# Joined later differences, a joined sixth product, sooner rows, high parts ahead of low parts, and a fourth row squared on two engines, in a hybrid decoder layer

## The chip, the core and the metric

The kernel runs on one core of one Trainium2 chip. The metric is device time in microseconds (us) of one execution; three timed runs of the kernel before gave 1316.51, 1317.4 and 1314.1 us, median 1316.51.

A core has five engines that run side by side, each through its own queue in order. PE (TensorE) multiplies and writes to PSUM banks; DVE (VectorE), ACT (ScalarE) and POOL (GpSimd) work on elements; SP (SyncE) issues most DMAs here. An instruction waits on semaphores for what it needs, and everything behind it on its engine waits with it. So the order in which the program gives instructions to each engine is part of the design.

## The reference

One decoder layer over 2048 positions of width 1024, in float32:

```python
xn = rms_norm(h, ln_g)
proj = jnp.einsum('bsd,de->bse', xn, w_in)            # 1024 -> 6 x 1024
b_gate, c_gate, x_conv, g_conv, x_lru, g_lru = jnp.split(proj, splits, axis=-1)
y_conv = short_conv_mixer(b_gate, c_gate, x_conv, conv_w)
y_conv = headwise_rms_norm(y_conv, N_CONV_HEADS, conv_out_g) * jax.nn.silu(g_conv)
y_lru = rg_lru_mixer(x_lru, lru_conv_w, lru_conv_b, w_a, b_a, w_i, b_i, lam)
y_lru = headwise_rms_norm(y_lru, N_LRU_HEADS, lru_out_g) * jax.nn.silu(g_lru)
y = jnp.concatenate([y_conv, y_lru], axis=-1)
h = h + jnp.einsum('bse,ed->bsd', y, w_out)           # 2048 -> 1024
return rms_norm(h, final_g)
```

`rg_lru_mixer` holds a width-4 convolution, two block-diagonal maps with sigmoids (the "gates") and a linear recurrence over the positions. Nearly all of the arithmetic is in the two projections.

## The kernel before

**Products.** Every float32 operand is split into a high part (a cast to fp32r, on ACT) and a low part (value minus high part, on DVE or POOL). A product of two 128x128-blocked operands is then three matmuls: high x high, high x low, low x high (`mm`, L1009). Each matmul has a 128x128 stationary piece S and a 128x512 moving piece T. Four such (index `j`, over 128 rows each) make one product of 12 matmuls.

**Steps.** `steps` (L268 to L272) lists 64 units of work, n = 0 to 63: for the first half of the positions (h = 0) 24 steps, kinds "l" (inputs of the recurrence), "a" and "b" (the convolution's), then 24 for the second half (h = 1), then 16 of kind "o" for the output projection. A step makes a 2x2 block of results by seven products in place of eight, with sums and differences of the blocks (indices 0 to 6). The S side of a step is prepared during the step before it by the eight small functions of `s_plan` (L192), called as `prep(n + 1, s - 1)`: index 6 of the list is `hi(5)`, the high part of product 5, which is called at the start of step n itself. Later halves load S again from DRAM by `s_loads`. The T side (differences of the x blocks, or of w_out's) lasts for a whole set of steps; sets open at n = 24, 48 and 56. The class `Change` (L435) builds the next set while the last steps of the old one run: `of_x` for n = 24, `of_w` for 48 and 56, one call per slot with a counter `q`. `sixth` (L473) makes the T operand of product 6 out of two earlier differences: DVE subtracts, `cut` casts on ACT and subtracts on DVE.

**Slots.** The loop at L1231 runs a step in seven slots of one product each, in the order 0, 6, 1, 3, 2, 4, 5, where the 6 is the sixth product of the step before (`pend`, L1296), added to a bank of that step. Products 0, 1, 2 and 5 add to one bank "A"; after products 0, 1 and 2 ACT copies the running sum out (L1315 `q1`, L1318 `u2`, L1321 `rr`), and the next product on "A" must wait for the copy. `put(which, bank, other)` consumes a finished block. The step that opens a set (n = 24, 48, 56) has eight plain products; the one after it (25, 49, 57, called `late`) has the order 0, 4, 5, 1, 3, 2 (`AFTER`). There are two ways to postpone: `at(k, f)` runs f at the k-th following `tick()`, that is at a slot's start, and `defer(f)` runs f at once unless `held[0]` is a list, in which case `release()` runs it (L175 to L184).

**The first three steps** have no seven products. Steps 0 to 2 use eight products each. Step 0 is written out by hand (L1101 to L1143): four rounds `j` for banks c11 and c21, then four for c12 and c22, while x is normalised (`norm_rows`, L528), turned by PE (`turn`, L550) and split. The first four rows of 128 positions are normalised before anything else, one after the other. Steps 1 and 2 are `plain(1, ...)` and `plain(2, ...)` (L1181), 8 slots each of 12 matmuls. `bits` (L1152) is a list of 16 small functions, four for each j: the first set's differences on DVE with casts on ACT. `after1` runs two of them in each slot of plain(1), all 16. `after2` in plain(2) would run those left over; it also prepares step 3 and, from slot 4 on, T operands 3 and 6.

**Around it.** Step 0's recurrence work is on timers that run through plain(1) and plain(2): `gates(0)` and then `sigs(0)` at the first slot of plain(2), `gates(1)` and `sigs(1)` at its third. A gate is two PSUM tiles of a pool with two buffers (`pss`), which ACT reads by four sigmoids (L758), so `gates(1)` must wait for `sigs(0)`. In "o" steps of the second kind (ph = 1) partial rows lie in DRAM (`od`) and are loaded (`load`, L891) by SP as `xr`, added on DVE (L942), squared on ACT (L931). `m1` (L830) is the first tap of the short convolution, on ACT.

Of the kernel before, what the change touches and what calls it, by code (L numbers as in the profile page):

```python
# [12 lines left out]
F32 = mybir.dt.float32  # L13
# [25 lines left out]
def hymba_kernel(ctx: ExitStack, tc: tile.TileContext, x, xt, w_in, par, lamc, w_gate, w_out, final_g, out):  # L39
# [152 lines left out]
    def s_plan(n, r, dst):  # L192
# [22 lines left out]
        def lo(i, eng=None):  # L215
            low(val(i), dst[i], eng)
            if PLAIN <= n < 3 * KT:
# [8 lines left out]
                lambda: (hi(4), lo(4, g), lo(2)),  # L226
                lambda: hi(5),
                lambda: (hi(6), lo(6, g), lo(5))]
# [206 lines left out]
    class Change:  # L435
# [36 lines left out]

        def sixth(self, *js):  # L473
            for j in js:
                tt(self.r[6, j], self.r[6, j], self.r[1, j], ALU.subtract)
            self.cut([(6, j) for j in js])

        def of_x(self, q):
# [13 lines left out]
            if q == 21:  # L492
                self.sixth(0, 1)
                at(1, lambda: self.sixth(2, 3))
            self.cut({1: ((5, 0), (5, 1)), 2: ((5, 2), (5, 3)), 4: ((0, 0), (0, 1)), 5: ((4, 0), (4, 1)),
# [31 lines left out]

    def norm_rows(b):  # L528
        junk = sp.tile([P, D], F32, tag="s", name="junk")
        ss = small.tile([P, 1], F32, tag="ss", bufs=4, name="ss")  # L530
        rs = small.tile([P, 1], F32, tag="rs", bufs=4, name="rs")
        nc.scalar.activation(out=junk, in_=x0[b], func=AF.Square, accum_out=ss)
        nc.scalar.activation(out=rs, in_=ss, func=AF.Sqrt, scale=1.0 / D, bias=eps)

        def scale():
            nc.vector.reciprocal(out=rs, in_=rs)
            nc.vector.tensor_scalar(out=x0[b], in0=x0[b], scalar1=rs, scalar2=0.0,
                                    op0=ALU.mult, op1=ALU.add)

        return scale  # L540
# [280 lines left out]
    def conv_a(h, k):  # L821
# [20 lines left out]
        def put(which, bank, other):  # L842
            if which in (11, 12):
                combine(p[:, 4:4 + C] if which == 11 else p[:, 4 + C:4 + N2], bank, other)
            else:
                xx[which] = aux("xx")
                combine(xx[which], bank, other)
            if which == 12:
                at(1, lambda: tt(p[:, 4 + C:4 + N2], p[:, 4 + C:4 + N2], xx[22], ALU.mult))
            if which == 21:  # L850
                tt(p[:, 4:4 + C], p[:, 4:4 + C], xx[21], ALU.mult)
                at(1, m1)
                at(2, lambda: mj(1), lambda: mj(2), keep)
# [30 lines left out]
    def outp(ph, m):  # L884
# [29 lines left out]
        elif ph == 1 or m not in X_LATE:  # L914
            at(5, lambda: load(0))
            at(6, lambda: load(1))

# [135 lines left out]
    with tc.manual_schedule(engines={ENG.PE, ENG.Activation, ENG.DVE, ENG.Pool, ENG.SP}):  # L1053
# [7 lines left out]
        Wr.append(load_s(1))  # L1061
        for b in range(NB):
            norm_rows(b)()
        Sp = [{} for _ in range(PLAIN)]

# [34 lines left out]
        Tp[0].lo(4)  # L1100
        c11, c21 = bank(), bank()  # L1101
        scale = lambda: None
        for j in range(NB):
            if j + 1 < NB:
                first(j + 1)
                for i in (0, 4):
                    Tp[j + 1].hi(i)
                Tp[j + 1].lo(0)
                Tp[j + 1].lo(4, g)
            scale()  # L1110
            scale = norm_rows(NB + j)
            for cc, aa in ((c11, 0), (c21, 2)):
                mm(cc, Sp[0], T, aa, j, j == 0, False, k=0)
# [18 lines left out]
        for j in range(NB):  # L1132
# [4 lines left out]
            if j == 2:  # L1137
                put = lru(0, 0, 1, 1)
                put(11, c11, None)
                put(21, c21, None)  # L1140
            for cc, aa in ((c12, 0), (c22, 2)):
                mm(cc, Sp[0], T, aa, j, j == 0, False, k=3)
# [51 lines left out]
        def after1(s):  # L1194
            i = {2: 2, 3: 3, 5: 0, 7: 1}.get(s)
            if i is not None:
                s_hi(2, i)
            do_bits(2)
            if i is not None:
# [13 lines left out]
        def after2(s):  # L1213
            do_bits(2)
            if s in (1, 2, 3, 4, 6, 7):
# [15 lines left out]
        for n in range(PLAIN, N):  # L1231
# [27 lines left out]
            bk = {}  # L1259
            slots = (0, 6) + ORDER[1:] if not late else AFTER  # L1260
            for s in range(6 if late else 8 if new or last else 7):
                i = slots[s]
                place[0] = {"l": 0, "a": 7, "b": 14}.get(kind, 0) + s
                tick()
                if soon and s == 3:
# [6 lines left out]
                if late:  # L1272
                    change.slot(16 + s)
                    if s == 0:
                        prep(n, 7)
                elif n > 0 and opens(n - 2):
# [3 lines left out]
                    elif s == 2:  # L1280
                        prep(n, 7)
                elif s == 0:
                    prep(n, 6)
                elif s == 2:
                    prep(n, 7)
# [5 lines left out]
                elif s > 0:  # L1291
                    held[0] = [] if i == 2 else None
                    prep(n + 1, s - 1)
                if s == 3:
                    load_next(n + 2, 3 if late else 4)
                if s == 1 and not late:  # L1296
                    if pend is not None:
# [15 lines left out]
                if i == 0:  # L1313
                    q1 = sm_q1[0] = sm("q1")
                    nc.scalar.copy(q1, bk["A"])  # L1315
                elif i == 1:
                    u2 = sm_u2[0] = sm(("u2", "rr")[n % 2])
                    nc.scalar.copy(u2, bk["A"])  # L1318
                elif i == 2:
                    rr = sm(("rr", "u2")[n % 2])  # L1320
# [3 lines left out]
                    if late:  # L1324
                        put(12, bk["D"], rr)
                elif i == 4:
                    put(11, bk["C"], q1)
# [54 lines left out]
```

## Time and profile before

| | us |
|---|---|
| median of three runs (range) | 1316.51 (1314.1 to 1317.4) |
| the profiled execution's own time | 1314.92 |
| its span on the core | 1313.1 |
| PE busy in the span | 1289.5 |
| DVE busy | 1046.0 |
| ACT busy | 748.7 |
| POOL busy | 250.0 |

The span is cut into stages by the steps: step 0 from about 14 to 45 us, plain(1) to 67 us, plain(2) to 98 us, then steps of about 20 us each; the sets open at about 513, 991 and 1148 us. In rows of the time view the columns are start, duration, engine, line, operation, tiles written<-read, shapes, count, and in brackets the idle time of the engine before the row with what ended it. In the view of waits the columns are the waiting engine, line and what it waited for, then total us, number of times and the longest. In the view of windows each stretch has, after its length, the busy us and count for PE, weight loads, DVE, ACT and POOL, then the granted clock, the DMA share and GB/s.

### The profile page before, as it was taken

To read this page: it belongs to the slowest core of one execution; us is meant where nothing else is said; L and a number is where in the kernel's file an instruction comes from. 1 tells how busy PE (TensorE), PEld (TensorE's weight loads), DVE (VectorE), ACT (ScalarE), POOL (GpSimd) and SP (SyncE) were. 2 spreads that over 40 slices of the span, in tenths; PEclk is the share of its full clock that TensorE was granted. 3 is DMA by queue.
4 is the path that set the end of the run, shared out by engine and by line. 5 is a ranking of instruction groups with operands and counts; after the bars stand their busy time and mean duration, and the time that the engine had idled before them with its cause. 6 is when DMAs were issued, how large, how long until landed. Compare 5 with 4: busy or idle time off the path is not lost.

```text
span 1313.1 us, 16711 instructions
## 1 busy us (share of the span) xinstructions
PE 1289.5 (98%) x5688; PEld 1061.0 (81%) x5688; DVE 1046.0 (80%) x1284; ACT 748.7 (57%) x1141; POOL 250.0 (19%) x189
## 2 busy tenths in 40 slices
PE   7989999999999999999999999999999999999997
PEld 6867888888888888778888888888888888887886
DVE  6789898999999998967666666667559767649886
ACT  7576767576675667566454645454466433445443
POOL 3204243344435441001010110101011000000000
PEclk9989999999999999999999999999999999999999
DMA  7128887898989887651899999999789986697654
GB/s 294 32 90 290 290 286 264 302 350 283 345 302 329 295 301 280 207 199 33 277 318 296 340 352 333 324 355 362 236 271 339 260 261 229 249 402 273 235 179 160
DMA packets 157958, 355.29 MB, mean 271 GB/s; under 512 B 16944, under 2 KB 51760, under 8 KB 157872
## 3 DMA queue, kind: packets, MB, share of 16 engines
q1 hardware_dynamic: 153264, 338.17, 74.4%
q0 software_dynamic: 4320, 15.73, 3.1%
q8 instruction: 45, 0.74, 0.2%
q14 instruction: 41, 0.34, 0.1%
q10 hardware_dynamic: 288, 0.32, 0.1%
HBM read 217.11 MB, written 137.04 MB: 270 GB/s over the span
## 4 chain that ended last, share of the span: by engine, by line
PE 82%; DVE 8%; DMA 5%; ACT 3%; issue 2%; SPq 0%; POOL 0%; ACTq 0%; DVEq 0%
PE bank L1014 79%; DMA s<-so 2%; DVE tl L163 2%; PE gate L751 2%; DVE traw L163 1%; DMA tl<-td 1%; DMA zr<-rsd 1%; DMA xr<-od 1%; DMA fg<-in_final_g_dram 1%; DVE u L723 1%; ACT i L758 0%; DVE s L163 0%; ACT r L758 0%; ACT th L451 0%; PE tp L554 0%
## 5 line engine op out<-in xcount | busy, mean ns | idle before, releaser
L1014 PE MATMUL bank<-th,s 128*128 128x512 f32 x3632 | 1129.6, 390 | 5.7 <-ACT rr L1318 1.6
L1014 PEld LDWEIGHTS bank<-th,s 128*128 128x128 f32 x3632 | 682.7, 188 | 151.7 <-ACT rr L1318 2.5
L1014 PE MATMUL bank<-tl,s 128*128 128x512 f32 x1816 | 708.2, 390 | 1.8 <-DVE tl L163 1.6
L1014 PEld LDWEIGHTS bank<-tl,s 128*128 128x128 f32 x1816 | 341.4, 188 | 74.5 <-DVE tl L163 3.0
L163 POOL TENSOR_TENSOR s<-raw,s 128x512 fp32r<-128x512 f32 x62 | 115.1, 1870 | 231.1 <-ACT s L213 176.0
L213 ACT CAST s<-raw 128x512 fp32r<-128x512 f32 x140 | 85.4, 618 | 48.4 <-PE bank L1014 32.8
L163 POOL TENSOR_TENSOR gb<-gb,sg 128x1024 f32<-128x1024 f32 x16 | 43.4, 2712 | 335.5 <-ACT sg L682 335.5
L163 DVE TENSOR_TENSOR s<-raw,s 128x512 fp32r<-128x512 f32 (+1 forms) x125 | 91.6, 755 | 10.6 <-ACT s L1073 6.7
L163 DVE TENSOR_TENSOR s<-s,s 128x512 fp32r<-128x512 f32 x105 | 86.6, 824 | 2.1 <-ACT s L213 1.5
L163 DVE TENSOR_TENSOR tl<-traw,th 128x512 fp32r<-128x512 f32 x85 | 60.8, 748 | 19.4 <-ACT th L451 13.4
L213 ACT CAST s<-s 128x512 fp32r<-128x512 f32 x105 | 64.7, 616 | 4.3 <-DVE s L163 4.0
L723 DVE SCALAR_TENSOR_TENSOR u<-xl,pt,u 128x1024 f32<-128x1024 f32 x48 | 61.3, 1278 | 6.1 <-ACT u L719 5.5
L835 DVE SCALAR_TENSOR_TENSOR t<-p,pt,t 128x1024 f32<-128x1024 f32 x32 | 46.5, 1454 | 16.6 <-ACT t L832 15.8
L1315 ACT COPY q<-bank 128x512 f32<-128x512 f32 x58 | 33.9, 584 | 40.9 <-PE bank L1014 31.5
L163 DVE TENSOR_TENSOR st<-u,st 64x512 fp32r<-64x512 f32 x64 | 53.8, 841 | 2.0
L758 ACT ACTIVATE r<-gate,pt 64x512 f32<-64x512 f32 x64 | 43.7, 683 | 17.3 <-PE gate L751 16.5
L1318 ACT COPY rr<-bank 128x512 f32<-128x512 f32 x31 | 18.1, 584 | 53.6 <-PE bank L1014 53.3
L1318 ACT COPY u<-bank 128x512 f32<-128x512 f32 x27 | 15.8, 585 | 52.4 <-PE bank L1014 52.4
L163 DVE TENSOR_TENSOR traw<-traw 128x512 f32<-128x512 f32 x60 | 41.8, 701 | 4.7 <-DMA traw<-in_w_out_dram 3.6
L451 ACT CAST th<-traw 128x512 fp32r<-128x512 f32 x64 | 36.1, 618 | 16.1 <-DVE traw L163 14.2
L758 ACT ACTIVATE i<-gate,pt 64x512 f32<-64x512 f32 x64 | 43.8, 684 | 1.1
L1321 ACT COPY u<-bank 128x512 f32<-128x512 f32 x31 | 18.1, 585 | 43.6 <-PE bank L1014 43.5
(169 smaller groups left out, 1294.1 us busy)
## 6 DMA issues: line engine op xcount, KB each, us to landing
sd<-s SPq DMA_DIRECT2D x151, 512.0 KB
s<-sd SPq DMA_DIRECT2D x151, 512.0 KB
raw<-in_w_in_dram SPq DMA_DIRECT2D x104, 256.0 KB
raw<-yd SPq DMA_DIRECT2D x64, 256.0 KB
traw<-in_w_out_dram SPq DMA_DIRECT2D x64, 256.0 KB
so<-so SPq DMA_DIRECT2D x22, 512.0 KB
s<-so SPq DMA_DIRECT2D x22, 512.0 KB
yd<-gl SPq DMA_DIRECT2D x32, 256.0 KB
```

Source lines behind the costliest of these rows:

```text
L163: (eng or nc.vector).tensor_tensor(out=out, in0=a, in1=b, op=op)
L213: nc.scalar.copy(dst[i][0], val(i))
L451: nc.scalar.copy(self.dst[i, j][0], self.r[i, j])
L723: nc.vector.scalar_tensor_tensor(out=v["u"], in0=o1[:, 1 + j:1 + j + N2], scalar=lw[j], in1=v["u"], op0=ALU.mult, op1=ALU.add)
L751: nc.tensor.matmul(ps[j], v["gw"][n][:, j, :], v["st"][j][:, sl], start=(n == 0), stop=(n == 1))
L758: nc.scalar.activation(out=g_[hi, sl], in_=v["ps"][j][src], func=AF.Sigmoid, bias=pt[src, bias + k:bias + k + 1])
L835: nc.vector.scalar_tensor_tensor(out=tcur["t"], in0=p[:, 2 + j:2 + j + N2], scalar=cw[j], in1=tcur["t"], op0=ALU.mult, op1=ALU.add)
L1014: nc.tensor.matmul(bank, a[:, js], b, start=start and n == 0, stop=stop and n == 2, skip_group_check=more)
L1315: nc.scalar.copy(q1, bk["A"])
L1318: nc.scalar.copy(u2, bk["A"])
L1321: nc.scalar.copy(rr, bk["A"])
```

## The change

- **Later differences.** `after1` runs `bits` only in its first six slots (12 of 16), and `after2` runs one in each slot, so the four of j = 3 run in the first four slots of plain(2).
- **Sixth product.** `sixth` does all four subtractions in one call at `q == 21`, and its cut one tick later. In step 26 the order of slots is 0, 3, 6, 1, 2, 4, 5. In "o" steps after an opening one, the slot's `Change` call moves behind the copy u2 where i = 1, and the preparation of the next step behind `put` where i = 2.
- **Deferred casts.** `hi(5)` and `m1` go through `defer`; a list is now open from the start of a step's first slot, and `release()` also follows the copies q1 and u2.
- **Sooner rows.** The two `xr` loads of step 56 (ph 1, m 2) are issued three ticks earlier.
- **High parts first.** In the first of the four rounds of each half of step 0, the 12 matmuls run in an order in which those that need only T's high parts come first (`spread`).
- **Fourth row.** Of the fourth row, DVE squares one half and ACT the other; the third and fourth rows are scaled in two parts, by column blocks, and the last part of the fourth on ACT, later.

```diff
-                lambda: hi(5),
+                lambda: defer(lambda: hi(5)),
...
-        def sixth(self, *js):
-            for j in js:
+        def sixth(self):
+            for j in range(NB):
                 tt(self.r[6, j], self.r[6, j], self.r[1, j], ALU.subtract)
-            self.cut([(6, j) for j in js])
+            at(1, lambda: self.cut([(6, j) for j in range(NB)]))
...
-                self.sixth(0, 1)
-                at(1, lambda: self.sixth(2, 3))
+                self.sixth()
...
+        if halves:
+            s2 = small.tile([P, 1], F32, tag="ss", bufs=4, name="s2")
+            nc.vector.scalar_tensor_tensor(out=junk[:, C:], in0=x0[b][:, C:], scalar=1.0, in1=x0[b][:, C:],
+                                           op0=ALU.mult, op1=ALU.mult, accum_out=s2)
+            nc.vector.tensor_scalar(out=s2, in0=s2, scalar1=1.0 / D, scalar2=EPS, op0=ALU.mult, op1=ALU.add)
+            nc.scalar.activation(out=junk[:, 0:C], in_=x0[b][:, 0:C], func=AF.Square, accum_out=ss)
+            nc.scalar.activation(out=rs, in_=ss, func=AF.Sqrt, scale=1.0 / D, bias=s2)
...
-                at(1, m1)
+                at(1, lambda: defer(m1))
...
-            at(5, lambda: load(0))
-            at(6, lambda: load(1))
+            sooner = 3 if ph == 1 and m == 2 else 0
+            at(5 - sooner, lambda: load(0))
+            at(6 - sooner, lambda: load(1))
...
-        for b in range(NB):
+        for b in range(NB - 2):
             norm_rows(b)()
+        third = norm_rows(NB - 2)
+        fourth = norm_rows(NB - 1, True)
+        third(0)
+        fourth(0)
+        third(1)
...
+        def spread(order):
+            seen = []
+            for cc, i, w, t, v in order:
+                nc.tensor.matmul(cc, Sp[0][i][w][:, 0:P], T[t, 0][v], start=not any(b is cc for b in seen),
+                                 stop=False)
+                seen.append(cc)
...
+                if j == 0:
+                    fourth(1)
...
+                spread(((c11, 0, 0, 0, 0), (c11, 0, 1, 0, 0), (c21, 2, 0, 0, 0),
+                        (c11, 1, 0, 4, 0), (c11, 1, 1, 4, 0), (c21, 3, 0, 4, 0), (c21, 2, 1, 0, 0),
+                        (c11, 0, 0, 0, 1), (c21, 2, 0, 0, 1), (c11, 1, 0, 4, 1), (c21, 3, 0, 4, 1),
+                        (c21, 3, 1, 4, 0)))
...
-            do_bits(2)
+            if s < 6:
+                do_bits(2)
...
-            do_bits(2)
+            do_bits(1)
...
+            if kind != "o" and n > 1 and opens(n - 2):
+                slots = (0, 3, 6, 1, 2, 4, 5)
...
+                if i == 1 and slots[2] == 6:
+                    held[0] = []
                 tick()
...
                 if late:
-                    change.slot(16 + s)
+                    if i != 1 or kind != "o":
+                        change.slot(16 + s)
...
                 elif s == 0:
+                    held[0] = []
                     prep(n, 6)
...
-                    held[0] = [] if i == 2 else None
-                    prep(n + 1, s - 1)
+                    if i == 2 and not late:
+                        held[0] = []
+                    if i != 2 or kind != "o" or not late:
+                        prep(n + 1, s - 1)
...
                     nc.scalar.copy(q1, bk["A"])
+                    release()
                 elif i == 1:
                     u2 = sm_u2[0] = sm(("u2", "rr")[n % 2])
                     nc.scalar.copy(u2, bk["A"])
+                    release()
+                    if late and kind == "o":
+                        change.slot(16 + s)
...
+                        if kind == "o":
+                            prep(n + 1, s - 1)
```

In the diff `fourth(1)` is the part of the scale that ACT runs (`activation` with Copy and the row's factor); `scale(part)` picks half of the column blocks.

More of the change, by code (lines that the diff above doesn't have):

```diff
@@ L525, in load, with norm_rows @@
             self.loaded = max(n, self.loaded)
-    def norm_rows(b):
+    def norm_rows(b, halves=False):
         junk = sp.tile([P, D], F32, tag="s", name="junk")
@@ L531, in norm_rows, with scale @@
         rs = small.tile([P, 1], F32, tag="rs", bufs=4, name="rs")
[L532 to L538, printed above, removed]
+        if halves:
[5 more added lines that the diff above has]
+            nc.scalar.activation(out=rs, in_=ss, func=AF.Sqrt, scale=1.0 / D, bias=s2)
+        else:
+            nc.scalar.activation(out=junk, in_=x0[b], func=AF.Square, accum_out=ss)
+            nc.scalar.activation(out=rs, in_=ss, func=AF.Sqrt, scale=1.0 / D, bias=eps)
+        def scale(part=None):
+            v = x0[b]
+            if part is not None:
+                v = v.rearrange("p (i k c) -> p i k c", i=2, c=P)[:, :, 2 * part:2 * part + 2, :]
+            if part != 1:
+                nc.vector.reciprocal(out=rs, in_=rs)
+            if part == 1 and halves:
+                nc.scalar.activation(out=v, in_=v, func=AF.Copy, scale=rs)
+            else:
+                nc.vector.tensor_scalar(out=v, in0=v, scalar1=rs, scalar2=0.0, op0=ALU.mult, op1=ALU.add)
         return scale
@@ L1111, in hymba_kernel @@
             scale = norm_rows(NB + j)
+            if j == 0:
+                spread(((c11, 0, 0, 0, 0), (c11, 0, 1, 0, 0), (c21, 2, 0, 0, 0),
+                        (c11, 1, 0, 4, 0), (c11, 1, 1, 4, 0), (c21, 3, 0, 4, 0), (c21, 2, 1, 0, 0),
+                        (c11, 0, 0, 0, 1), (c21, 2, 0, 0, 1), (c11, 1, 0, 4, 1), (c21, 3, 0, 4, 1),
+                        (c21, 3, 1, 4, 0)))
+                continue
             for cc, aa in ((c11, 0), (c21, 2)):
@@ L1140, in hymba_kernel @@
                 put(21, c21, None)
+            if j == 0:
+                spread([(cc, i, w, t, 0) for t, d in ((3, 0), (5, 1)) for cc, i in ((c12, d), (c22, 2 + d))
+                        for w in range(2)] +
+                       [(cc, i, 0, t, 1) for t, d in ((3, 0), (5, 1)) for cc, i in ((c12, d), (c22, 2 + d))])
+                continue
             for cc, aa in ((c12, 0), (c22, 2)):
@@ L1291, in hymba_kernel @@
                 elif s > 0:
-                    held[0] = [] if i == 2 else None
-                    prep(n + 1, s - 1)
+                    if i == 2 and not late:
+                        held[0] = []
+                    if i != 2 or kind != "o" or not late:
+                        prep(n + 1, s - 1)
                 if s == 3:
                     load_next(n + 2, 3 if late else 4)
-                if s == 1 and not late:
+                if i == 6 and not late and s < 3:
                     if pend is not None:
```

## The prediction

> **What bounds the kernel now.** I read the page first: busy shares, then the chain.
>
> ```profile
> PE 1289.5 (98%) x5688; PEld 1061.0 (81%) x5688; DVE 1046.0 (80%) x1284; ACT 748.7 (57%) x1141; POOL 250.0 (19%) x189
> ```
>
> PE works almost throughout, and the change leaves the number of matmuls as it is. So the only time to win is PE's idle time. The chain in order of time gives the undisturbed pace, and two windows give a slow stretch and a stretch full of transfers:
>
> ```profile
> 141.75 51.71 PE bank L1014 x228
> ```
>
> ```profile
> 73.42:83.99 10.57, 6.97 (x16) 4.84 (x16) 8.46 (x12) 10.00 (x17) 0.10 (x1) 0.68 0.01 2
> ...
> 1150.00:1170.00 20.00, 20.00 (x90) 16.57 (x89) 6.49 (x10) 7.55 (x15) 0.53 (x1) 1.00 1.04 405
> ```
>
> A 128x512 matmul costs 51.71 / 228 = 0.227 us. The first window holds 16 matmuls, worth 16 x 0.227 = 3.6 us, in 10.57 us: **6.9 us lost in one place**, part of it idle, part at a granted clock of 0.68.
>
> PE's waits, asked for in four stretches, say where the rest is (0 to 45, 45 to 105, 545 to 575 and, in the last fence, 1020 to 1030 and 1175 to 1195):
>
> ```profile
> PE tp L554 <- DVE x L537: 2.9, 3, 1.8
> PE spin L548 <- POOL ident masks.py:199: 1.6, 1, 1.6
> PE bank L1014 <- DVE tl L163: 1.4, 3, 0.9
> PE bank L1014 <- ACT th L261: 0.4, 1, 0.4
> PE bank L1014 <- ACT th L1124: 0.4, 1, 0.4
> PE bank L1014 <- POOL tl L163: 0.2, 1, 0.2
> ```
>
> ```profile
> PE gate L751 <- ACT i L758: 3.6, 2, 3.4
> PE bank L1014 <- ACT q L1315: 0.7, 1, 0.7
> ```
>
> ```profile
> PE bank L1014 <- DVE xx L163: 1.3, 1, 1.3
> PE norm_ps L627 <- ACT i L758: 0.8, 1, 0.8
> PE bank L1014 <- DVE tl L163: 0.2, 1, 0.2
> PE bank L1014 <- ACT th L451: 0.2, 1, 0.2
> ```
>
> ```profile
> PE bank L1014 <- ACT rr L1318: 0.3, 1, 0.3
> ...
> PE bank L1014 <- ACT rr L1318: 1.3, 1, 1.3
> PE bank L1014 <- DVE ob L163: 1.1, 1, 1.1
> ```
>
> A stop costs more than its idle time. Around the wait for q:
>
> ```profile
> 100.35 0.39 PE L1014 MATMUL bank<-th,s 128*128 128x512 f32 x1
> 101.47 0.50 PE L1014 MATMUL bank<-th,s 128*128 128x512 f32 x1 [0.73 <-ACT q L1315]
> 101.80 0.40 PE L1014 MATMUL bank<-tl,s 128*128 128x512 f32 x1
> ```
>
> From the first start to the third are 1.45 us where two matmuls take 0.45: 1.0 lost for 0.73 idle. I add 0.27 us to each stop.
>
> **The change part by part.**
>
> *Term B, later differences.* ACT's rows ahead of the gates' sigmoids:
>
> ```profile
> 70.56 0.59 ACT L814 COPY p<-bank 128x512 f32<-128x512 f32 x1
> 73.17 0.62 ACT L1160 CAST th<-traw 128x512 fp32r<-128x512 f32 x1 [2.02 <-DVE traw L163]
> ...
> 75.15 0.58 ACT L814 COPY xx<-bank 128x512 f32<-128x512 f32 x1
> 75.62 0.68 ACT L758 ACTIVATE r<-gate,pt 64x512 f32<-64x512 f32 x1
> ```
>
> The cast of L1160, and a second one in the rows left out, belong to j = 3 of `bits`. They wait for DVE, and the sigmoids that free the two gate tiles wait behind them. The change moves both casts and DVE's six operations of j = 3 into plain(2). Then ACT goes from 70.56 + 0.59 = 71.1 straight on with one cast of S (0.62, like this one) and the copy xx (0.58): sigmoids from 72.3, the first gate tile free at 73.7, the second at 75.1. PE reaches `gates(1)` where the first window begins, at 73.5, and still waits for each: products go on at about 75.8 in place of 74.4 (four gate matmuls after 73.5), so 1.4 of the 6.9 remain. What is late next: the moved work makes ACT in plain(2) fuller, and by my count of its queue (two casts more, and m1, tanh, exp and the square root in the same order) it reaches the copy q of step 3 some 0.5 later than PE, beside the 0.73 already there, since that copy stands directly between two products. No DMA moves with `bits`; T operands 1 to 3 and 6 of j = 3 are done some 2 us ahead of their first use. B = 6.9 - 1.4 - 0.5 = **5.0**; 3.0 if ACT's new queue is as slow as the old one by half, 6.4 if the gates wait for nothing.
>
> The Trainium skill (TensorE: Matmul & The Clock Gate, part 1) says that the clock falls to half after one idle window of about 3.4 us, and that these windows run freely. The wait here is 3.4 us long, just at that length, and the 0.68 shows that this execution met it. By that rule other executions of before might escape it, and B would then be 3.0 and the sum 10.8; a wait of 1.4 stays clear of it either way.
>
> *Term C, set at step 24.* PE waits for `xx`, which frees the bank of the sixth product; xx waits for rr, and rr for ACT:
>
> ```profile
> 552.88 1.23 ACT L451 CAST th<-traw 128x512 fp32r<-128x512 f32 x2 [4.37 <-DVE traw L163]
> 554.01 0.58 ACT L1321 COPY u<-bank 128x512 f32<-128x512 f32 x1
> ```
>
> ACT sat 4.37 us in front of the first half of the sixth's cast while the copy rr stood behind it. Joined, the four subtractions run on DVE while ACT takes rr; the four casts come a slot later, and the order 0, 3, 6, 1 gives them one more product, 12 x 0.227 = 2.7 us. Lost before: 2.5 idle + 4 stops x 0.27 = 3.6. New: with 1 and 2 adjacent on bank A, the copy u2 stands bare. The nearest case is the copy q above, 1.0 per stop, less the four norm_ps matmuls that now fall between (0.45): 0.6. Behind m1, which now waits for u2, stand the taps on DVE, a slot later; PE needs their result only in `put` of the next slots. S of product 3 is needed two slots sooner, but its load was issued a step before. C = 3.6 - 0.6 = **3.0**; 1.5 if the bare copy costs 1.0 and T6 comes 1 us late, 3.3 if norm_ps hides it.
>
> *Terms D and E, sets 48 and 56.* At 1027 the wait for rr goes, since the copy now precedes the cast: 0.3 + 0.27 = **0.6** (at least 0.3). At 1183 and 1190 the waits are 2.4 + 2 x 0.27 = 2.9. DVE's waits from 1160 to 1180:
>
> ```profile
> DVE ob L163 <- DMA xr<-od: 7.7, 2, 4.8
> DVE tl L163 <- ACT th L451: 6.9, 1, 6.9
> DVE raw L163 <- DMA zr<-rsd: 0.3, 1, 0.3
> ```
>
> DVE stood 7.7 us for these rows while cuts, raw x zr and `put` queued behind. Three ticks earlier is 3 x 2.7 = 8.2 us, more than either wait. But the DMA share is 1.04 at 405 GB/s there, so sooner rows are paid by others in SP's queue: two loads of 512 KB, 1.3 us each at that rate, move past four tl<-td of 256 KB and two s<-so, and the second also past the yd and rsd loads of step 58. PE shows no wait for a T or S operand in that stretch, and the 6.9 above is DVE ahead of its work, so tl and s have room; zr already comes 0.3 too late, so 1.3 more makes DVE wait some 1.6 for it, far less than 7.7. E = **2.9**; 1.0 if DVE then waits for those loads instead.
>
> *Term A, start.* DVE scales the second and the fourth row at:
>
> ```profile
> 8.44 0.75 DVE L537 TENSOR_SCALAR x<-x,rs 128x1024 f32<-128x1024 f32 x1
> ...
> 11.08 0.75 DVE L537 TENSOR_SCALAR x<-x,rs 128x1024 f32<-128x1024 f32 x1
> ```
>
> ```profile
> L723 DVE SCALAR_TENSOR_TENSOR u<-xl,pt,u 128x1024 f32<-128x1024 f32 x48 | 61.3, 1278 | 6.1 <-ACT u L719 5.5
> ```
>
> The trace has no square with a sum on DVE. Bounds for the half: half of L723's 1.28 and the whole of it; I take 0.7, since the row's form is the same and the size half. For half a scale, 0.38 to 0.75; I take 0.45. DVE, free at 8.44 + 0.75 = 9.2: 0.7, then three steps on single columns of some 0.2 each, and two halves: 9.2 + 0.7 + 0.6 + 0.9 = 11.4 to 11.5 in place of 11.83, a gain of 0.3 (a loss of 0.8 with both upper bounds). The other halves run beside PE's transposes. High parts first: the waits for tl (1.4 in three stops, 0.2 in one) lose 1.6 + 4 x 0.27 = 2.7. But what comes late next is near. In the first round the fourth matmul needs T4's high part, one ACT cast later; in the second, POOL's low part stands close:
>
> ```profile
> 18.41 1.28 POOL L163 TENSOR_TENSOR tl<-traw,th 128x512 fp32r<-128x512 f32 x1 [3.67 <-ACT th L261]
> ```
>
> It ends at 19.7, and PE needs it 0.9 after its round's start, which would now be 17.6. So I count 1.0 of the 2.7. `fourth(1)` puts 0.6 on ACT ahead of casts; between nothing and 0.6, counted in those ends. A = 0.3 + 1.0 = **1.3**, between 0.2 and 2.6.
>
> The Trainium skill (VectorE: DVE Perf Modes, the TRN2 errata) says that each instruction from SBUF pays a fixed time, so two halves cost more than a whole. By its table, (58 + 256) cycles at 0.96 GHz, an estimate from that page, a half takes 0.33 and the whole 0.59. The row has 0.75 for the whole, so its fixed part here is larger. By the page the sum would be 0.1 lower.
>
> Sum: 1.3 + 5.0 + 3.0 + 0.6 + 2.9 = **12.8** (6.0 to 15.8 from the ends). The profiled execution took 1314.92, with 1313.1 in the span: 1302.1 by it. The median is 1.6 higher: 1303.7. I say **1303**.
>
> **The rivals.**
>
> 1. *The waits come back one step later.* For: DVE has 80% of the span, a DMA share of 1.04 at step 56, and the gates' wait is on an engine whose queue only shifts. Against: DVE's and ACT's own idle rows above. Each term at its low end: 1316.5 - 6.0 = 1310.5. Chance 0.20.
> 2. *Before without the half clock.* In the window, 6.9 splits into some 5 for waits and 2 for nine or ten matmuls that take twice 0.227 at the lower clock. Where runs of before do not fall, the gain is 2 smaller: 1303 + 2 = 1305. The Trainium skill's rule, above, lets it come and go. The trace shows it fallen once. Chance 0.07.
> 3. *Slower: the deferred cast.* hi(5) now waits in ACT's queue for q, and what follows there comes 0.62 later, in 33 steps (21 of h = 0, 2 of h = 1, 10 of kind "o").
>
> ```profile
> L1318 ACT COPY rr<-bank 128x512 f32<-128x512 f32 x31 | 18.1, 584 | 53.6 <-PE bank L1014 53.3
> ```
>
> If all of it lands on PE: 33 x 0.62 = 20 us, 1316.5 - 12.8 + 20 = 1324; it decides from 0.4 us per step. Against: ACT is idle 53.3 / 31 = 1.7 us before the next copy, so it is hidden. Chance 0.04.
>
> That the change does nothing is excluded for B: the casts leave the queue ahead of the sigmoids.
>
> **How the numbers follow.** Forecast 0.69, rivals 0.20, 0.07, 0.04. The range takes all terms' high ends (1314.9 - 15.8 = 1299.1) and the first rival's end, a little widened below: 1298.5 to 1310.5. What a measurement can tell from no change is 0.3%, 4 us, so faster is below 1312.6: the forecast, the second rival and nearly all of the first, 0.93. Within 0.3%: 0.03; slower: 0.04.
>
> **What would show it.** B: sigmoids at 72 to 73 us, PE's gate waits 1.0 to 1.5 in sum, granted clock 1.00 there. C: the waits for xx and norm_ps gone, one for u2 of 0.3 to 0.8. D, E: no waits for rr and ob, DVE's wait for xr under 1 us, a small one for zr. A: first product at about 13.5, and short waits for th and POOL's tl. Wrong if the view of PE's waits shows gate waits above 3, new waits in the steps between 110 and 500 us, or a wait for zr of several us.

## The result and the profile after

| | before | after |
|---|---|---|
| median, runs side by side (us) | 1316.09 (1314.1 to 1317.4) | 1303.78 (1302.7 to 1304.65) |
| ratio after / before, with its 95% interval | | 0.9907 (0.9894 to 0.9921) |
| the profiled execution and its span (us) | 1314.92, 1313.1 | 1302.7, 1300.9 |

The changed kernel is 12.3 us faster by the medians and 12.2 by the two spans; 1303 was forecast. Of all the runs told of here one was slow: a run of e5_fourth took 2642.39 us, and it counts in that kernel's median (1304.08 without it) but in no ratio. The head of the page, with the busy times by engine:

```profile
span 1300.9 us, 16699 instructions
...
PE 1285.6 (99%) x5688; PEld 1059.9 (81%) x5688; DVE 1042.9 (80%) x1288; ACT 748.7 (58%) x1142; POOL 247.8 (19%) x189
```

PE has the same 5688 matmuls and is busy 3.9 us less (1289.5 before, where those at half clock took longer). Everything that was won lies in PE's idle time and in its clock. PE's waits over the whole span (what it waited for, then us in total, times, longest):

```profile
PE tp L567 <- DVE x L551: 1.7, 2, 1.1
...
PE bank L1028 <- ACT u L1374: 1.2, 1, 1.2
PE bank L1125 <- ACT th L261: 1.1, 1, 1.1
PE bank L1028 <- ACT q L1364: 0.7, 1, 0.7
PE gate L764 <- ACT i L771: 0.7, 1, 0.7
PE bank L1125 <- ACT th L1159: 0.4, 1, 0.4
PE bank L1028 <- ACT u L1368: 0.2, 1, 0.2
...
PE bank L1028 <- POOL tl L163: 0.2, 1, 0.2
```

Against the list of before: the gates 0.7 in place of 3.6, the transposes' wait for x 1.7 in place of 2.9, the waits for xx, norm_ps, rr L1318, ob and DVE's tl gone, q and the th of a later round (L1159) as they were. One row is new and large: 1.2 for "u L1374", which is the copy that runs after product 2 (L1321 before). One has grown: the first product's wait for th, from 0.4 to 1.1.

To put sizes to the stages I added up, over PE's rows, what each start-to-start distance exceeds the pace (0.227 us for a 512-wide matmul, 0.110 for the short transposes and sums):

| stage (us from the start) | lost before | lost after | gained | forecast |
|---|---|---|---|---|
| 0 to 50: A | 10.0 | 9.0 | 1.0 | 1.3 |
| 50 to 150: B | 8.9 | 4.3 | 4.5 | 5.0 |
| 500 to 600: C | 3.8 | 0.7 | 3.1 | 3.0 |
| 1000 to 1050: D | 0.7 | 0.4 | 0.3 | 0.6 |
| 1150 to 1200: E | 3.0 | 0.2 | 2.8 | 2.9 |
| all others | 1.6 | 1.1 | 0.5 | 0 |
| sum | 27.9 | 15.7 | 12.2 | 12.8 |

So B, C and E came near their places and sizes, A and D came smaller, and 0.5 of the 12.2 came where nothing was forecast. B is read from three groups of rows of the time view (start, us, engine, line, operation). The gates first:

```profile
70.07 0.63 ACT L1092 CAST s<-raw 128x512 fp32r<-128x512 f32 x1
70.60 0.60 ACT L827 COPY xx<-bank 128x512 f32<-128x512 f32 x1
71.07 0.69 ACT L771 ACTIVATE r<-gate,pt 64x512 f32<-64x512 f32 x1
...
72.51 0.50 PE L764 MATMUL gate<-st,bh 128*128 128x512 f32 x1
...
73.91 0.50 PE L764 MATMUL gate<-st,bh 128*128 128x512 f32 x1 [0.67 <-ACT i L771]
...
74.48 0.39 PE L1028 MATMUL bank<-th,s 128*128 128x512 f32 x1
```

The sigmoids start at 71.07 in place of 75.62. The first gate tile is free before PE arrives at 72.51; only the second stops it. From 72.51 to the next product at 74.48 are 1.97 us for four matmuls: 1.06 lost. The windows show the clock:

```profile
72.00:78.00 6.00, 5.33 (x23) 3.86 (x22) 4.27 (x6) 5.90 (x10) 0.10 (x1) 1.00 0.01 3
78.00:84.00 6.00, 6.00 (x28) 4.99 (x27) 5.91 (x11) 5.12 (x9) 0.00 (x0) 1.00 0.21 87
```

The granted clock is 1.00 in both; before, the window from 73.42 to 83.99 had 0.68. Of the 6.9 lost here 5.8 are gained. But 32 us later something is given back:

```profile
99.87 3.38 POOL L163 TENSOR_TENSOR gb<-gb,sg 128x1024 f32<-128x1024 f32 x1
...
100.92 2.88 DVE L163 TENSOR_TENSOR s<-raw 128x512 f32<-128x512 f32 x1
...
103.83 0.69 DVE L163 TENSOR_TENSOR s<-s,raw 128x512 f32<-128x512 f32 x1
...
104.56 0.62 ACT L213 CAST s<-s 128x512 fp32r<-128x512 f32 x1 [2.47 <-DVE s L163]
...
105.09 1.05 ACT L586 ACTIVATE xrow<-xrow 128x1024 f32<-128x1024 f32 x1
...
105.19 0.39 PE L1028 MATMUL bank<-th,s 128*128 128x512 f32 x1
...
106.14 0.56 ACT L1374 COPY u<-bank 128x512 f32<-128x512 f32 x1
...
106.75 0.50 PE L1028 MATMUL bank<-th,s 128*128 128x512 f32 x1 [1.18 <-ACT u L1374]
107.09 0.39 PE L1028 MATMUL bank<-tl,s 128*128 128x512 f32 x1
```

Read it upwards from the end. PE waits 1.18 for a copy; from 105.19 to 107.09 are 1.90 us where two matmuls take 0.45, so 1.45 are lost. ACT reached the copy late, because it stood 2.47 for a sum of S on DVE with a square of 1.05 behind. And DVE's sum took 2.88 us where the same shape takes 0.69 in the next row, while POOL's product of gb and sg ran. DVE ended 0.55 after POOL did (103.80 against 103.25). This is where B lost its half microsecond against the forecast, and more. The copy isn't a bare one: between product 2, whose sum it takes, and product 5, which waits for it, stands the whole of product 4 with its 2.7 us, and the copy came too late even for that.

### The profile page after: what moved, and what is told of

It is laid out like the page before. It is cut to its first block, busy times and chain, and to the rows that moved or that the text cites. A ratio compares the mean times of both kernels' runs of the same rounds, so it can differ in the third digit from the quotient of the medians.

```text
span 1300.9 us, 16699 instructions
## 1 busy us (share of the span) xinstructions
PE 1285.6 (99%) x5688; PEld 1059.9 (81%) x5688; DVE 1042.9 (80%) x1288; ACT 748.7 (58%) x1142; POOL 247.8 (19%) x189
## 4 chain that ended last, share of the span: by engine, by line
PE 90%; DVE 2%; ACT 1%; issue 0%; DVEq 0%
PE bank L1028 88%; PE gate L764 2%; DVE s L163 1%; DVE tl L163 0%; DVE ob L163 0%; DVE r L798 0%; ACT th L1262 0%; DVE ob L990 0%; ACT L783 0%; DVE xr L163 0%; ACT r L783 0%; ACT s L213 0%; ACT xrow L586 0%; DVE u L163 0%; DVE u L789 0%
## 5 line engine op out<-in xcount | busy, mean ns | idle before, releaser
L163 DVE TENSOR_TENSOR s<-raw,s 128x512 fp32r<-128x512 f32 (+1 forms) x125 | 88.7, 732 | 10.5 <-ACT s L1092 6.6
L163 DVE TENSOR_TENSOR raw<-raw,zr 128x512 f32<-128x512 f32 x64 | 41.1, 683 | 7.3 <-DMA zr<-rsd 7.1
L1374 ACT COPY u<-bank 128x512 f32<-128x512 f32 x31 | 18.1, 584 | 46.2 <-PE bank L1028 46.0
(180 smaller groups left out, 1300.9 us busy)
```

The lines of the kernel that those rows point to most:

```text
L163: (eng or nc.vector).tensor_tensor(out=out, in0=a, in1=b, op=op)
L1374: nc.scalar.copy(rr, bk["A"])
```

## The experiments

Each kernel is the changed one with one edit. The times were taken beside runs of the kernel before on the same chip, and the ratios' intervals reach 1.8 to 2.6 us to either side; only those of e1_bits and e3_sets lie clear of the changed kernel's. The differences in the text are those of the medians; by the ratios each kernel comes out 0.2 to 1.2 us higher against the changed one. What is smaller than the intervals is read from the traces.

| run | time (us) | ratio to before, 95% | span |
|---|---|---|---|
| changed kernel | 1303.78 | 0.9907 (0.9894 to 0.9921) | 1300.9 |
| e1_bits | 1308.60 | 0.9950 (0.9935 to 0.9964) | 1307.8 |
| e2_sooner | 1305.71 | 0.9928 (0.9913 to 0.9943) | 1305.3 |
| e3_sets | 1308.92 | 0.9954 (0.9939 to 0.9968) | 1306.8 |
| e4_spread | 1305.28 | 0.9927 (0.9907 to 0.9946) | 1302.5 |
| e5_fourth | 1304.15 | 0.9911 (0.9893 to 0.9928) | 1301.7 |
| e6_defer | 1304.05 | 0.9916 (0.9900 to 0.9933) | 1301.4 |
| e7_third | 1303.03 | 0.9906 (0.9891 to 0.9921) | 1301.0 |
| e8_silu | 1301.92 | 0.9896 (0.9881 to 0.9911) | 1299.8 |
| e10_both | 1301.67 | 0.9896 (0.9879 to 0.9914) | 1299.7 |
| e11_seven | 1305.63 | 0.9930 (0.9911 to 0.9948) | 1303.6 |

One thing disturbs single traces: near 710 us PE waits for a load of S in some executions (2.0 us in e1_bits, 0.2 to 0.4 in e3_sets, e4_spread, e5_fourth and e10_both, nothing in the changed kernel's trace or in before's). No edit is near it, and it is left out below.

### e1_bits: the differences as before (B undone)

```diff
-            if s < 6:
-                do_bits(2)
+            do_bits(2)
```

> The changed kernel with all 16 pieces of the first differences back in plain(1). My theory: the casts of j = 3 again stand ahead of the gates' sigmoids, so PE's wait for the gate goes from 0.7 us back to about 3.5 and the clock falls again; the new wait of 1.2 us for the copy rr of step 3 (at 105 us) goes, since it came from the work moved into plain(2). Net about +4.5 us, near 1308. Rival, the clock: if a wait of this length misses the clock's fall, only about +2.5 us, with a granted clock of 1.00 between 73 and 84 us. Rival, shift: if the wait at step 3 stays, it has nothing to do with the moved work.

Measured: 4.8 us slower than the changed kernel. PE's waits, and the windows behind its two longest stops:

```profile
PE gate L764 <- ACT i L771: 3.6, 2, 3.5
...
PE bank L1028 <- DMA s<-sd: 2.0, 1, 2.0
```

```profile
78.00:84.00 6.00, 6.00 (x17) 4.71 (x17) 5.13 (x6) 5.82 (x10) 0.10 (x1) 0.59 0.01 3
716.00:722.00 6.00, 4.00 (x18) 2.96 (x17) 3.95 (x6) 3.62 (x5) 0.00 (x0) 1.00 1.06 383
```

Both effects are back at the old place, the wait and behind it a clock of 0.59: 17 matmuls in 6 us, where 26 fit. The wait for the copy "u L1374" is gone. So the old order costs 6.0 us between 50 and 100 us and saves 1.4 between 100 and 150: the new wait at 105 us belongs to the same edit, as the other side of it. Behind the 2.0 us stop at 716 us the clock stays at 1.00.

POOL's product and DVE's work on S meet in the old order too:

```profile
105.98 2.85 POOL L163 TENSOR_TENSOR gb<-gb,sg 128x1024 f32<-128x1024 f32 x1
106.49 2.88 DVE L163 TENSOR_TENSOR s<-s,s 128x512 fp32r<-128x512 f32 x1
```

But here the first sum had run at 103.45 in 0.69, and what stood still was a low part that no cast ahead of the copy needs; ACT had been idle for 1.62 when PE's product 2 let it start the copy (109.08). Counted from the copy q of step 3, POOL's product starts at about the same time in both kernels (6.0 us here, 6.1 in the changed kernel), DVE's first sum at 3.5 here and at 7.2 in the changed kernel. So the change did not make the meeting: the differences moved into plain(2) made DVE later, and the first sum ran into it.

### e11_seven: half of it

```diff
-            if s < 6:
+            if s < 7:
```

> Half of the part that the first experiment undid: the second plain row makes 14 of its 16 differences before the gates instead of 12 (all 16 there gave a gate wait of 3.5 us and a clock at half speed behind it). The first sigmoid should start near 73.8 us (71.07 with 12, 74.77 with 16), so the gates wait 2.2 to 2.7 us instead of 0.7 and lose 1.5 to 2.0 more. Theory (the clock falls behind a stop of TensorE that is long enough; it fell behind 3.4, 3.5 and 2.5 us and stayed behind 2.0 and 1.4 us): the wait lies at the edge; with full clock some 1305.5, with the half clock some 1308. Rival (the clock falls for something else at this place, whatever the wait, so any kernel with the old order shows it): 1308 and half clock even with a wait under 2.0.

Measured: 1.9 us slower than the changed kernel. PE's rows and the window behind them:

```profile
75.17 0.50 PE L764 MATMUL gate<-st,bh 128*128 128x512 f32 x1 [2.48 <-ACT i L771]
75.50 0.40 PE L764 MATMUL gate<-st,bl 128*128 128x512 f32 x1
76.57 0.64 PE L764 MATMUL gate<-st,bh 128*128 128x512 f32 x1 [0.67 <-ACT i L771]
77.01 0.63 PE L764 MATMUL gate<-st,bl 128*128 128x512 f32 x1
```

```profile
78.00:84.00 6.00, 6.00 (x24) 4.84 (x23) 5.93 (x8) 5.14 (x9) 0.10 (x1) 0.82 0.00 0
```

The sigmoids came at 73.74 and the wait was 2.48, as expected. The number 1305.5 was met for a wrong reason: the clock did fall, from 76.6 to 80.0 us, and stage B lost 4.2 more between 50 and 100, but the wait at 105 us went as well and gave 1.6 back. After the two gate matmuls at full speed, each later one took 0.427 from start to start. The clock fell behind stops of 3.4 (before), 3.5 (e1_bits), 2.5 (here) and 2.5 us (e2_sooner, at 1174 us), and stayed behind 2.0 and 1.4.

The length of one stop is not all that counts, though. In the traces' clock records every stretch of one clock between its first and last change lasts a multiple of 3.41 us: 3.41 at half clock here and in e2_sooner, 6.83 in before and e1_bits. In the 3.41 us ahead of these four falls PE started no matmul (before, e1_bits) or three (here, e2_sooner) of the 15 that fit at the pace. The stop of 2.0 us in e1_bits lies across two such pieces, and in the emptier one eight started. And in e4_spread the clock fell at 10.74 us, behind 3.41 us whose longest stop was 0.73 but in which only 12 short (128-wide) matmuls started. So it fits these runs that the clock goes by how much PE does in each piece, and where a stop lies against the pieces would count as well as its length; a stop of the same length at another place was not tried.

### e2_sooner: the rows of step 56 as late as before (half of E undone)

```diff
-            sooner = 3 if ph == 1 and m == 2 else 0
+            sooner = 0
```

> The changed kernel with the partial rows of step 56 loaded at their old ticks. My theory: DVE again stands some 7 us for xr, and PE waits again at steps 57 and 58: 1.0 to 2.4 us of idle time between 1150 and 1195, +1.3 to +2.9 us, near 1306. Rival, order: the copy u2 moved ahead of the cut is what removed both waits; then PE has under 0.3 us of waits there and the time stays at 1304.

Measured: 1.9 us slower by the medians, within what was expected; the runs reach from 1304.5 to 1307.1, and the profiled one is the slowest, so the trace shows the edit at its worst. DVE's waits between 1155 and 1185, PE's longest wait, and a window:

```profile
DVE ob L163 <- DMA xr<-od: 9.0, 2, 4.8
```

```profile
PE bank L1028 <- ACT rr L1368: 2.5, 1, 2.5
```

```profile
1174.00:1180.00 6.00, 3.45 (x9) 2.60 (x9) 5.93 (x11) 2.77 (x5) 0.53 (x1) 0.72 1.02 345
```

DVE stands 9.0 us for xr, the sums of S behind it are late, so are ACT's cast and the copy rr in its queue, and PE stops for 2.5. In the changed kernel's trace neither wait is there and the clock stays at 1.00. In this execution the order alone, without sooner rows, wins nothing of E (4.3 lost at this stage, 3.0 before); by the medians it would keep some 0.9 of the 2.8.

### e3_sets: the sixth product in two halves and the old orders (C, D and the other half of E undone)

```diff
-        def sixth(self):
-            for j in range(NB):
+        def sixth(self, *js):
+            for j in js:
...
-            at(1, lambda: self.cut([(6, j) for j in range(NB)]))
+            self.cut([(6, j) for j in js])
...
-                self.sixth()
+                self.sixth(0, 1)
+                at(1, lambda: self.sixth(2, 3))
...
-            if kind != "o" and n > 1 and opens(n - 2):
-                slots = (0, 3, 6, 1, 2, 4, 5)
```

The `change.slot` and `prep` calls of late "o" steps stand ahead of the copies again, too.

> The changed kernel with the sixth product's operand made in two halves again, the old order of slots in step 26 and the old order around the copies in steps 49 and 57. My theory: the waits of 2.5 us in four stops near 545 us come back (about +3.1 us) and the one of 0.3 near 1015 (+0.6), in all +3.7 us, near 1307.5. Rival, backlog: if a large part of the gain there came from DVE and ACT arriving with less work behind them after the other parts, PE's waits there stay under 1.5 us and the time under 1306.

Measured: 5.1 us slower. PE's waits:

```profile
PE bank L1029 <- DVE xx L163: 1.4, 1, 1.4
...
PE norm_ps L641 <- ACT i L772: 0.8, 1, 0.8
PE bank L1029 <- DVE ob L163: 0.8, 1, 0.8
PE bank L1029 <- ACT rr L1365: 0.7, 2, 0.5
```

The same four waits as before stand at the same sets. More is lost than in the changed kernel by 3.2 at step 24, 0.4 at step 48 and 1.4 at step 56. With e2_sooner: the sooner rows alone win 1.4 of E (3.0 lost before, 1.6 here), the order alone nothing in e2_sooner's one trace.

### e6_defer: hi(5) and m1 at once

```diff
-                lambda: defer(lambda: hi(5)),
+                lambda: hi(5),
...
-                at(1, lambda: defer(m1))
+                at(1, m1)
...
-                    held[0] = []
...
-                    release()
```

> The changed kernel with the cast hi(5) and the tap m1 issued at once again. My theory: in the 33 steps the cast is hidden either way, so PE has no new wait between 110 and 500 us and the time moves by less than 0.5 us, but for step 26, where m1 ahead of the copy u2 may lengthen PE's wait of 0.2 us to about 0.8. Rival: the deferral costs in each step (time falls by 1 us or more) or gains in each step (time rises by 1 us or more).

Measured: 0.3 us slower than the changed kernel, too little to tell. Between 110 and 500 us PE has no wait in either kernel, so the cast's place costs nothing in the even steps. At step 26 the one wait grows from 0.2 to 0.8 (PE's waits from 535 to 575 us):

```profile
PE bank L1028 <- ACT u L1366: 0.8, 1, 0.8
```

That is 0.6 us, by stage too (1.2 lost against 0.6): the deferral serves the bare copy of C and nothing else that shows.

### e4_spread and e5_fourth: the two halves of A undone

e4_spread takes away both `spread` calls, so that the first rounds run in the old order; e5_fourth gives the fourth row back to ACT and its scales, whole, to DVE.

```diff
-        for b in range(NB - 2):
+        for b in range(NB):
             norm_rows(b)()
-        third = norm_rows(NB - 2)
-        fourth = norm_rows(NB - 1, True)
-        third(0)
-        fourth(0)
-        third(1)
```

> The changed kernel with the first rounds of step 0 in the old order, high by low second. My theory: the first product starts at 13.9 us in both kernels before and after, so the whole gain of about 1.0 us in the first 45 us is that of the order; PE waits for DVE's low parts again, about 1.3 us in three or four stops, and the time rises by 1 to 2 us. Rival: the fourth row gave it, and this changes the time by less than 0.3 us.

> The changed kernel with the fourth row squared and scaled whole again. My theory: the four rows then reach PE 0.7 us later, but the first product still starts at 13.9 us, since in the changed kernel DVE runs the second part of the third row, slowed to about 1.4 us beside POOL, ahead of the first turned block. Time within 0.4 us of the changed kernel. Rival: first product at 14.5, and 0.6 us slower.

Measured: e4_spread is 1.5 us slower by the medians, 0.5 by the stage from 0 to 50 us (9.5 lost against 9.0); the ratios' intervals overlap. The trace does not size the order cleanly, because its granted clock was 0.50 from 10.74 to 14.15 us, where the changed kernel had 1.00. The 13 transposes ahead of the first product took 2.80 in place of 1.63:

```profile
11.65 2.80 PE L567 MATMUL tp<-ident,x 128*128 128x128 f32 x13
```

The first product therefore started at 14.21 in place of 13.91, which is 0.3 of the 0.5. From there the first round took 3.89, against 3.22 with the high parts first and 4.56 in the kernel before; of the 0.67 between the first two only 0.2 is left at the end of the stage. The old order's stops for low parts come back, shorter than in the kernel before (PE's waits from 12 to 20 us):

```profile
PE bank L1028 <- DVE tl L163: 0.5, 2, 0.2
```

e5_fourth, which keeps the order and drops the split, is the same as the changed kernel within 0.4, as expected, and loses 9.2 from 0 to 50 us, where the kernel before loses 10.0. Its start tells more. The first product in e5_fourth, and the rows that lead to it in the changed kernel:

```profile
13.59 2.24 PE L1120 MATMUL bank<-th,s 128*128 128x512 f32 x7 [0.41 <-ACT th L261]
```

```profile
10.64 1.90 DVE L551 TENSOR_SCALAR x<-x,rs 128x512 f32<-128x512 f32 x2
...
10.92 2.75 POOL L163 TENSOR_TENSOR s<-raw,s 128x512 fp32r<-128x512 f32 x2 [8.54 <-ACT s L1092]
...
12.46 0.74 DVE L574 TENSOR_SCALAR traw<-tp,pt 128x512 f32<-128x512 f32 x1
...
13.91 2.24 PE L1125 MATMUL bank<-th,s 128*128 128x512 f32 x7 [1.09 <-ACT th L261]
```

Without the split the first product starts 0.3 *sooner*. With it, DVE has two half scales in the row at 10.64: 1.90 us for the two, of which the first takes 0.49. The second starts inside POOL's first product and ends some 0.3 after it, at 12.54; the first turned block (12.46, each start slightly overlaps the end before it) stands behind it in DVE's queue. The 0.7 that PE's transposes gain (the last one starts at 12.55, in the kernel before at 13.26) is lost again in the wait for th.

### e7_third: that half moved to ACT

```diff
-            if part == 1 and halves:
+            if part == 1:
...
-        third(1)
...
                 if j == 0:
+                    third(1)
                     fourth(1)
```

> The changed kernel with the second part of the third row's scale on ACT, beside the fourth's, and no longer on DVE. My theory: DVE takes the first turned block at once, and the first product starts near 13.2 us in place of 13.9: 0.5 to 0.7 us faster. Rival: ACT's 0.7 us more delays the casts of the second round (ACT had 0.6 us idle there), and the gain is under 0.2 us.

Measured: the mechanism is as expected, the gain is not. The first product:

```profile
13.25 2.24 PE L1124 MATMUL bank<-th,s 128*128 128x512 f32 x7 [0.41 <-ACT th L261]
```

It starts 0.66 sooner, but stage A loses only 0.2 less (8.8 against 9.0): the low parts' four matmuls behind it now take 1.28 in place of 1.08, and the next round starts slower too. The rival (a gain under 0.2) was nearly right: 0.8 by the medians, nothing by the spans.

### e8_silu: the first SiLU product on DVE

In the step that consumes the convolution's first blocks, gb x sg runs on DVE instead of POOL.

```diff
-                silu(g)
+                silu(g, 0, nc.vector if h == 0 and k == 0 else None)
```

> The changed kernel with the first product gb x sigmoid of the convolution on DVE in place of POOL. Theory for the new wait at 105 us: ACT's copy rr stands behind a cast that waits for DVE's first sum of step 4, and that sum took 2.9 us in place of 0.7 beside POOL's product. Without POOL there the sum takes 0.7, the wait of 1.2 us goes, and the kernel is 1.0 to 1.4 us faster. Rival: DVE's 1.2 us for the product takes the same place, and the wait stays above 0.5 us.

Measured: 1.9 us below the changed kernel by the medians, 1.1 by the spans. DVE's and ACT's rows at the same place:

```profile
100.84 0.68 DVE L163 TENSOR_TENSOR s<-raw 128x512 f32<-128x512 f32 x1
...
102.28 0.62 ACT L213 CAST s<-s 128x512 fp32r<-128x512 f32 x1 [0.27 <-DVE s L163]
...
103.87 0.57 ACT L1374 COPY u<-bank 128x512 f32<-128x512 f32 x1
103.97 1.22 DVE L163 TENSOR_TENSOR gb<-gb,sg 128x1024 f32<-128x1024 f32 x1
```

The sum of S is back at 0.68, the copy comes 2.27 sooner, and PE's wait of 1.2 is gone. DVE took on 1.22 us of work and the kernel became faster: the product on POOL had cost DVE 2.19 (2.88 - 0.69). A wait of 0.4 for gates at 127 us is new, part of what the span does not gain.

### e10_both: the two fixes together

> The two edits that each shortened a wait, together: the third row's second scale on ScalarE, and the first SiLU product of the conv on VectorE instead of GpSimd. Theory (an operation of VectorE with two inputs in SBUF, or a scale, that meets a GpSimd product stands still until that product ends; both edits take a meeting away, at different places): the gains add, first product near 13.2 us, no wait of step 3's copy at 105 us, and the time is 0.2 to 0.4 below the kernel with the SiLU product alone, so 1301.5 to 1301.7, some 2.2 below the changed kernel. Rival (the sooner start only moves the work against the weights' transfers and is given back at a later wait): the same as the SiLU product alone, 1301.9 or more.

Measured: 1301.67, 2.1 below the changed kernel. First product at 13.33, no wait at 105 us. Against e8_silu alone 0.25 us is less than these runs tell apart; all runs of both (up to 1302.55) lie below all of the changed kernel (from 1302.70), though the ratios' intervals overlap.

## Why the prediction was right

The forecast was 1303 and the sum 12.8; measured were 1303.78 and 12.2. Of the 12.2, 11.7 came from the five places named. That the sum is so near is in part luck: within B one term came better than said and another worse, and 0.5 came from stages with no term. By its own steps:

- **What bounds.** Right: PE's idle time and clock held all of it. The 0.27 added to each stop held again (1.45 lost for 1.18 idle at 105 us).
- **B, the gates.** Right, and 0.3 better than said. I put the sigmoids at 72.3, after the cast of S and the copy xx from 71.1. ACT took that cast at 70.07, straight behind the copy p, and was done at 71.07, so one of the two stops fell away: 1.06 in place of 1.4. e1_bits shows that the edit does it.
- **B, "what is late next".** Here the step failed in its term: "it reaches the copy q of step 3 some 0.5 later". That wait stayed at 0.7. Late was the copy after product 2, and it cost 1.45. I counted ACT's queue and put nothing down for DVE's, where the moved operations made the first sum of S later by some 3.6 us (7.2 behind the copy q, 3.5 in e1_bits). There it met a product on POOL and stood still until this ended; without that product the wait is gone (e8_silu). Net B = 6.9 - 1.06 - 1.45 = 4.4, by the stages 4.5.
- **C.** Right: 3.1 for 3.0; the copy u2 costs 0.2 idle and some 0.4 with its stop, where 0.6 was said. The deferral is part of it (0.8 idle without it, e6_defer); what the norm_ps matmuls hide was not tried.
- **D.** 0.3 for 0.6, at its stated low end, in this trace. One trace doesn't size it: with D's edit in place the stage loses 0.04 to 0.06 in seven of the experiments' traces, 0.4 in e2_sooner and 0.7 in e4_spread.
- **E.** 2.8 for 2.9. That sooner rows are paid by others was right in kind and too small in size. DVE's wait between 1155 and 1185 us:

```profile
DVE raw L163 <- DMA zr<-rsd: 4.5, 1, 4.5
```

I had said 1.6 for zr, and had named a wait for zr of several us as a sign of being wrong in the view of PE's waits. PE shows none there: the wait took the place of 7.7 + 0.3 on DVE, which still stands 3.5 us less. The whole of E needed both halves; the rows alone won half of it (e3_sets).

- **A, fourth row.** This term failed: "a gain of 0.3" at the first product. It started at 13.91 as against 13.94. The halves alone are as costed (0.68 for the square, 0.49 for a scale; 0.7 and 0.45 were said), but one of them met POOL and took 1.50, and the turned block waited behind it. The sentence that the sum would be 0.1 lower with halves of 0.33 has its sign wrong: halves shorter than the 0.45 taken would make the gain larger.
- **A, high parts first.** 1.0 was said. Kept without the split it wins 0.8 by the trace (e5_fourth); undone it costs 1.5 by the medians, and 0.5 by a trace whose clock fell (e4_spread). So its size stays open between these. The waits left are the forecast ones, th and POOL's tl of 0.2.
- **Rivals.** The waits one step later: only the one at 105 us came, 1.45 of the 6.8 that this rival gave back. Before without the half clock: the mean granted clock of the 20 runs of before beside the experiments is 0.994 to 0.997 in 18 and 0.998 in two (1313.07 and 1315.02 us), and in the changed kernel's five runs 0.998 or 0.999. So a lower clock is usual in before, not an accident of the profiled execution, and e1_bits shows the fall again behind the same wait; whether two runs escaped it is not shown. The split of the 6.9 was off: from 77.05 to 83.99 before starts 15 matmuls, 3.4 us at the pace, in 6.9 us, so about 3 were the clock's after the stops are taken off, not 2. The deferred cast: no PE wait between 110 and 500 us, and putting it back gains nothing.

The Trainium skill (SBUF — State Buffer, who interferes with whom) says that GpSimd and a VectorE instruction with two inputs in SBUF, or a scale in a fast mode, take turns for a shared port, and that the second "fully blocks". The collisions here agree: the operations on S ended 0.55 after POOL's product at 103.25, and in e1_bits 0.55 after one at 106.02 and 0.55 after one at 108.83. Taken into the prediction, the rule would have made one ask, for each moved DVE operation, what POOL does at that time.

## What to carry to other kernels

When work is moved on one engine, follow it to each copy that a product waits for, also one with a whole product of room, and ask there of every engine ahead of the copy how much later it gets, not only of the one that copies. Ask also whether an operation of DVE will lie beside one of POOL: a sum of S of 0.69 then ended 0.55 after POOL's product in each case here. A stop of the matmul engine of 2.5 us can cost more than its length: in e11_seven and e2_sooner the clock fell behind it and took some 1.5 to 1.7 us on top, and about 3 behind the 3.4 us of before; so shorten the longest stops first. Undo the parts of a joint change one at a time: of E's two halves one alone won 1.4 and the other nothing in its trace, and undoing B's edit tied the new wait at 105 us to it.

## What the runs showed of the hardware that was not expected

- A 128x512 sum on DVE took 2.88 us beside a 1024-wide product on POOL, 0.69 alone; a half scale took 1.50 (0.49 alone). It works both ways: POOL's product took 3.38, as DVE's row ahead of it ended only at 100.99.
- A sum output on DVE's square is an instruction of its own, 0.08 us after 0.68 for 512 columns.
- The granted clock fell behind stops of 2.48 and 2.55 us and not behind 2.00, and in e4_spread behind stops of 0.73 at most among short matmuls. In the 3.41 us ahead of each fall PE had started three 512-wide matmuls or none, or 12 128-wide ones. In e2_sooner the first matmul after the stop was already slow, in e11_seven it was the third. Matmuls then start 0.427 apart, for 3.4 us in each of these two, and for 6.9 behind the longer stops of before (77.05 to 83.99) and e1_bits.
